# Moving sums of weights made in DRAM from the MLP into the attention, their copies issued by ScalarE, and two more direct pieces in the wide group

## The chip, the cores and the metric

The kernel runs on one NeuronCore of a Trainium2 chip. The core has five engines with an instruction stream each: TensorE (PE, matrix products into PSUM), VectorE (DVE), ScalarE (ACT), GpSimd (POOL) and SyncE (SP). An engine works through its own stream in the order in which it was written, and waits where an instruction needs something that another engine or a transfer has not finished. Sixteen DMA engines move data between DRAM and the on-chip memory SBUF, or from DRAM to DRAM; a transfer is issued by an instruction in the stream of SP, ScalarE or GpSimd. The metric is the time of one execution on the device in microseconds (us), as the median of several runs.

## The reference

One layer of an encoder on 256 tokens plus 16 meta tokens (272 rows, width 2048), all in float32:

```
h    = concat(meta_tokens, x)                                  # 272 x 2048
proj = rmsnorm(h) @ w_in                                       # 8 heads of neighbourhood attention + latent q, kv, rope key
out_a = neighbourhood_attention(q, k, v, bias)                 # 8 heads of 128
out_b = mla_attention(rmsnorm(cq) @ w_q_up, rmsnorm(ckv) @ w_kv_up, rope key)   # 8 heads
h    = h + concat(rmsnorm(out_a), rmsnorm(out_b)) @ w_out
y    = rmsnorm(h)
g    = conv3(y @ w_gate) + conv_b                              # depthwise over positions; 5632 columns
h    = h + (silu(g) * (y @ w_up)) @ w_down                     # 5632 -> 2048
return h[16:]                                                  # 256 x 2048
```

Every weight is read from DRAM once. The weights of `w_in`, `w_out`, `w_gate`, `w_up` and `w_down` are what streams through the chip.

## The kernel before, in words

**Products.** TensorE multiplies in a shortened float32 format (fp32r). So each weight piece is split by ScalarE into a rounded part (`whi`, L249, `split_hi`) and by VectorE into the rest (`wlo`, L253, `split_lo`), and an ordinary product is three matmuls: high by high, high by low, low by high (`mm3`, L712 to L714). In the up projection and in most of the direct down projection two instructions do the same work (`mm2`, L2035 and L2036).

**Pieces.** All weights form one list, `pieces`, in the order in which TensorE uses them. A piece is up to 128 x 1024 floats (512 KB). `load_weights` walks the list on SP's queue: it waits until one of a few raw buffers is free, and issues the load (L542). Then ScalarE splits, VectorE splits and frees the raw buffer, and TensorE uses the four high and four low buffers in turn. Pieces 0 to 15 belong to the compressed projections, then 16 pieces to each of four pairs of heads, then 32 to `w_out`, then the MLP. Piece 14 is the last but one of the first `w_in` columns, and piece 48 the first of the third pair of heads.

**Seven products for eight.** Parts of the MLP use a scheme of Strassen's kind: a 2 x 2 block product out of seven block products, where some factors are sums of weight quarters and some are sums of activation quarters. It is used for five groups of four column tiles of `w_up` (`QUADS`, 256 columns a product), for the first 1024 columns of `w_down` (the wide group, 512 columns a product, 22 row pairs of 21 matmuls each) and for the next 512 columns (the mid group, 256 columns a product). The remaining 512 columns of `w_down` are direct: four column tiles of six pieces each, 24 direct pieces, the last of each tile half as long.

The weight sums are mostly made by VectorE (`weight_sums`, L253 on `raw` and `halves`). For the wide group a part of them is made in DRAM: for each of the 22 row pairs `early` holds a DRAM buffer, one source to copy and one to add. The function `sums_in_dram` first copies the one source into the buffer, DRAM to DRAM (L542, on SP), then adds the other with an adding DMA issued by GpSimd (L781). Even pairs have 512 KB, odd ones 256 KB. When the wide group comes, these sums are loaded like weights (`early_sums`). `mlp_buffers` starts `sums_in_dram` when the MLP begins; a copy is issued each time round the loop and an addition two rounds behind it, and the loop then lets `EARLY_PACE`, 15 us of the plan's time, go by.

**Order of work.** The instruction streams are written by a planner inside the kernel (`Flow`). Each thread of work (a Python generator) asks for an engine and says how long it will hold it; the planner always takes the request that can start first, and so writes down one order for all engines. `yield "sp", 600` is such a request, `Event` and `Slots` are its waits. `dma_free` is the planner's idea of when the transfers are through. Only the order goes into the program. `fl.cur.t += x` moves the thread's planned time on, so its next request comes at least x ns later in the plan.

**Order of the MLP.** `work` lists the MLP's pieces: gate and up pieces with the five quads between them; then the mid group between the last gate and up pieces; then `TAIL`, a string of `m` (a row pair of the mid group) and `d` (a direct piece); then the wide group's units with direct pieces spread between them; and last, `BEHIND` direct pieces after the wide group. While the last ones run, `scheme_out` puts the wide group's seven results together on ScalarE, VectorE and GpSimd and writes them out.

Of the kernel before, what the change touches and what calls it, by code (L numbers as in the profile page):

```python
# [12 lines left out]
ALU = mybir.AluOpType  # L13
AX = mybir.AxisListType

P = 128
# [45 lines left out]
GATE_PRIO = 2  # L62
LENT = 14
MID_SUMS = 0
EARLY_PACE = 15000.0
LANDING, SAVING = 2600.0, 2500.0
BEHIND = 4
MID_LEAD, TAIL = 4, "mmdmmddddmmdddd"
LAST = FC // 2 - 1


# [145 lines left out]
def encoder_block(ctx: ExitStack, tc: tile.TileContext, io):  # L217
    nc = tc.nc
    ctx.enter_context(tc.manual_schedule())
    fl = Flow()  # L220
# [8 lines left out]
    def tiles(pool, n, shape, name, dt=F32):  # L229
        return [pool.tile(shape, dt, tag=f"{name}{i}", name=f"{name}{i}") for i in range(n)]  # L230


    def size(ap):
        n = 1
        for s in ap.shape[1:]:
            n *= s
        return n
# [194 lines left out]
    pieces = []  # L432
# [79 lines left out]
    def spread(a, b):  # L512
        out = []
        for i, u in enumerate(a):
            j, k = (t * len(b) // len(a) for t in (i, i + 1))
            out += [u] + b[j:k]
        return out
# [11 lines left out]
    work += [(left if c == "m" else ahead).pop(0) for c in TAIL]  # L529
    n = len(others) - BEHIND  # L530
    work += spread(scheme, others[AHEAD:n])
# [3 lines left out]
    dma_free = [0.0]  # L535

    def load(out, src, ev, queue):

        nc_bytes = 4 * P * size(out)
        t = max(dma_free[0], fl.cur.t) + nc_bytes / 350.0  # L540
        dma_free[0] = t
        queue.dma_start(out, src)  # L542
        fl.set(ev, t + (2000.0 if fl.cur.t < 4e5 else LANDING) - fl.cur.t)
# [3 lines left out]
    def load_piece():  # L547
        p = pieces[n_loads[0]]
        n_loads[0] += 1
        if isinstance(p, Quarters):  # L550
            if p is p.pair.pieces[0]:
                yield from load_pair(p.pair)
            return
        p.raw = yield from one(raws)
        yield "sp", 600
        load(p.raw[:, : p.n], p.src, p.loaded, nc.sync)
# [90 lines left out]
    def load_weights():  # L647
        while n_loads[0] < len(pieces):
            yield from load_piece()
# [102 lines left out]
    early_sums, early_mid, early = [], [], []  # L752
    for g in range(0, FC // 2 if MID_SUMS else 0, MID_SUMS or 1):
        n = min(MID_SUMS, FC // 2 - g)
        t = dpool.tile([P, n, PW // 4], F32, name=f"early_m{g}")
        w = io["w_down_m"][g : g + n].rearrange("g p c -> p g c")
        q, ev = PW // 4, Event()
        early.append((t, w[:, :, :q], w[:, :, 2 * q : 3 * q], ev))
        early_mid += [(t[:, i], ev) for i in range(n)]
    for g in range(FC // 2):  # L760
        ev, q, w = Event(), PW // 2, io["w_down_s"][g]
        if g % THIRD:
            t = dpool.tile([P, q], F32, name=f"early{g}")
            early.append((t, w[:, q : 2 * q], w[:, 2 * q : 3 * q], ev))
        else:
            t = dpool.tile([P, PW], F32, name=f"early{g}")
            early.append((t, w[:, : 2 * q], w[:, q : 3 * q], ev))
        early_sums.append((t, ev))

    def sums_in_dram():  # L770
        copied = [Event() for _ in early]
        for i in range(len(early) + 2):
            if i < len(early):
                t, src, _, _ = early[i]
                yield "sp", 600
                load(t, src, copied[i], nc.sync)
            if i >= 2:
                t, _, src, done = early[i - 2]
                yield copied[i - 2]
                yield "pool", 1000  # L780
                nc.gpsimd.dma_start(t, src, accum_op=ALU.add)  # L781
                dma_free[0] = max(dma_free[0], fl.cur.t) + 8 * P * size(t) / 350.0
                fl.set(done, 8000.0)
            fl.cur.t += EARLY_PACE

    late = [hpool.tile([P, 2, L], F32R, tag=f"late{i}", name=f"late{i}") for i in range(8)]
# [11 lines left out]
    def first_loads():  # L798
        k, first = 0, pieces[0]
        for n, weights in ((1, 1), (1, 1), (2, 2), (3, 2), (2, 1), (2, 1), (4, 2)):  # L800
            t = x_tiles[k // 8][:, k % 8 : k % 8 + n]
            yield "sp", 450
            ev = Event()
            load(t, io["xT"][:, k : k + n, :], ev, nc.sync)
            for i in range(n):
                xt[k], x_gain[k], ev_x[k] = t[:, i, :L], t[:, i, L:], ev
                k += 1
                fl.set(ev_xt[k - 1])
            if k == 1:
                yield "sp", 450  # L810
                part = first.parts[1]
                load(first.raw[:, part], first.src[:, part], first.there[1], nc.sync)
                k = 2
            for _ in range(weights):
                yield from load_piece()
        yield "sp", 600
        load(vecs, io["vecs"], ev_vecs, nc.sync)
        fl.spawn(load_weights())
        yield pieces[9].loaded
        yield "sp", 600  # L820
        load(consts, io["consts"], Event(), nc.sync)
        yield "sp", 600
        load(ident, io["ident"], ev_consts, nc.sync)
        yield "sp", 600
        load(mb, io["meta_bias"], Event(), nc.sync)

    def load_residual():
        yield ev_ob[HEADS - 1]
        for i in range(8):
            t = hpool.tile([P, 2, NT], F32, tag=f"late{i}", name=f"res{i}")  # L830
            yield "sp", 600
            hT[2 * i], hT[2 * i + 1] = t[:, 0, :], t[:, 1, :]
            load(t, io["xT"][:, 2 * i : 2 * i + 2, :NT], ev_res[i], nc.sync)
# [286 lines left out]
    for h in range(HEADS):  # L1120
        t = apool.tile([P, 2, NT], F32R, name=f"ob{h}")
        ob.append((t[:, 0, :], t[:, 1, :]))
        t = apool.tile([P, 2, NT], F32R, name=f"oa{h}") if h < 6 else hl[KC - HEADS + h]
# [647 lines left out]
    def attention_weights():  # L1771
# [76 lines left out]
        for parts, evs, evac in ((ob, ev_ob, out_b), (oa, ev_oa, out_a)):  # L1848
            for g in range(8):
# [7 lines left out]
                for c in range(2):  # L1857
                    fl.spawn(evac(2 * g + c, pss[c]))
        fl.spawn(scale_h())
        fl.spawn(mlp_buffers())  # L1860
        yield from mlp_weights()

# [4 lines left out]
    act = mts = None  # L1867

    def mlp_buffers():

        nonlocal act, mts
        yield ev_s2t
        yield ev_resT
        actx.close()
        mpool = ctx.enter_context(tc.tile_pool(name="mpool", bufs=1))
        act = mpool.tile([P, FC, 2, SEQ], F32R, name="act")
        mts = Slots(tiles(mpool, 12, [P, NT], "mt"))
        for t in tiles(mpool, 2, [P, PW], "sin"):
            fl.put(s_parts, t)
        for t in tiles(mpool, 1, [P, PW], "more_raw"):  # L1880
            fl.put(raws, t)
        for b in banks[4:]:
            fl.put(acc, b)
        for i in range(KC // 2):
            f = FC - KC + 2 * i
            near[i] = act[:, f : f + 2].rearrange("p f i t -> p (f i t)").bitcast(F32)
        fl.set(ev_mlp)
        fl.spawn(sums_in_dram())
        for i, (dst, saved) in enumerate(saved_sums["up"][:EARLY]):
            yield saved  # L1890
            yield "sp", 600
            load(near[i], dst, ev_near[i], nc.sync)
# [335 lines left out]
    def scheme_out(sums7):  # L2228
# [34 lines left out]
        fl.spawn(done(1, 0))  # L2263

    fl.spawn(first_loads())
    fl.spawn(make_gains())

# [171 lines left out]
```

## Time and profile before

| What | Value |
|---|---|
| Time, median of 3 runs | 1115.56 us (1112.71 to 1118.1) |
| The profiled execution: its time, its span | 1116.94 us, 1114.8 us |
| TensorE, VectorE, ScalarE, GpSimd busy | 1102.8, 1015.9, 751.8, 142.8 us |
| Moved by DMA | 265.35 MB, mean 238 GB/s |
| Attention and output projection | up to about 392 us |
| MLP with the five quads | about 397 to 784 us |
| Mid group, with the last gate and up pieces | about 784 to 950 us |
| Wide group | about 960 to 1098 us |
| First and last DRAM copy issued | 400.3 and 768.1 us |
| First and last DRAM addition issued | 407.1 and 776.7 us |

The span runs from the first to the last instruction, and the time of an execution is a little longer. Busy means that an instruction of the engine was under way; matmuls overlap, so the mean duration of one is longer than the distance to the next. In the groups' rows, `out<-in` are the program's names, `x` the count, and after the bar stand the busy time and the mean duration in ns. `[1.74 <-DMA raw<-in_w_up_s]` behind an instruction is the time that its engine stood idle before it, and what ended that. In waits, `A <- B: 7.0, 6, 2.0` means that A waited for B 7.0 us in all, 6 times, 2.0 us at the longest. SPq, ACTq and POOLq are the engines' instruction streams where they issue transfers.

### The profile page before, as it was taken

What the parts mean: (1) busy time and instruction counts of PE and PEld (TensorE: products, weight loads), DVE (VectorE), ACT (ScalarE), POOL (GpSimd) and SP (SyncE); (2) the same over time, 40 slices, a digit from 0 to 9 for tenths busy, and PEclk for the clock granted to TensorE, in tenths of its full rate; (3) what the DMA queues carried; (4) which work ended last, traced back from release to release, by engine and by line L of the source; (5) the groups of instructions that cost most, each with busy time, mean ns of one, the idle gap of its engine ahead of it and who ended that gap; (6) DMA issues with size and microseconds to landing.
All of it is one profiled execution on the core that took longest, in us unless ns stands there. A gap on an engine that the chain in (4) does not pass through costs nothing.

```text
span 1114.8 us, 22339 instructions
## 1 busy us (share of the span) xinstructions
PE 1102.8 (99%) x8164; PEld 1049.1 (94%) x8164; DVE 1015.9 (91%) x1922; ACT 751.8 (67%) x1514; POOL 142.8 (13%) x217
## 2 busy tenths in 40 slices
PE   9999999999999999999999999999999999999998
PEld 9999999999999999999999999999999999887777
DVE  7979888888878989999999999999999989899997
ACT  8788989898647786556656556666665665676664
POOL 3211222121332300000000000000000000310011
PEclk9999999999999999999999999999999999999999
DMA  9653434444655689778868878889889879698891
GB/s 318 197 174 121 151 123 156 139 155 140 225 185 171 216 308 306 250 244 244 288 196 268 253 239 267 284 253 316 296 295 304 269 271 360 241 316 298 296 315 75
DMA packets 82470, 265.35 MB, mean 238 GB/s; under 512 B 9304, under 2 KB 13016, under 8 KB 82360
## 3 DMA queue, kind: packets, MB, share of 16 engines
q1 hardware_dynamic: 78600, 254.08, 66.9%
q0 software_dynamic: 3472, 9.57, 4.9%
q8 instruction: 64, 1.05, 0.4%
q14 instruction: 46, 0.38, 0.1%
q10 hardware_dynamic: 288, 0.27, 0.1%
HBM read 245.39 MB, written 35.13 MB: 252 GB/s over the span
## 4 chain that ended last, share of the span: by engine, by line
PE 62%; DVE 21%; DMA 7%; ACT 5%; issue 4%; POOL 0%; SPq 0%; DVEq 0%; ACTq 0%; POOLq 0%
PE bank L289 14%; DVE wlo L253 12%; PE bank L714 11%; PE bank L712 11%; PE bank L713 11%; PE bank L2035 8%; PE bank L2036 4%; DMA raw<-in_w_up_s 3%; ACT whi L249 3%; DVE raw L253 2%; PE bank L295 2%; DVE mt L253 2%; DMA halves<-early 1%; DVE halves L253 1%; DVE mt L261 1%
## 5 line engine op out<-in xcount | busy, mean ns | idle before, releaser
L249 ACT ACTIVATE whi<-raw 128x512 fp32r<-128x512 f32 (+2 forms) x512 | 381.5, 766 | 159.9 <-PE bank L713 48.1
L253 DVE TENSOR_TENSOR wlo<-raw,whi 128x512 fp32r<-128x512 f32 (+2 forms) x512 | 443.5, 885 | 33.1 <-ACT whi L249 31.7
L712 PE MATMUL bank<-hl,whi 128*128 128x258 f32 (+1 forms) x1208 | 348.5, 289 | 0.1
L714 PE MATMUL bank<-hl,wlo 128*128 128x258 f32 (+1 forms) x1208 | 345.1, 286 | 1.4 <-DVE wlo L253 1.3
L713 PE MATMUL bank<-hl,whi 128*128 128x258 f32 (+1 forms) x1208 | 344.3, 285 | 0.0
L714 PEld LDWEIGHTS bank<-hl,wlo 128*128 128x128 f32 x1208 | 230.4, 191 | 3.5 <-DVE wlo L253 2.9
L713 PEld LDWEIGHTS bank<-hl,whi 128*128 128x128 f32 x1208 | 230.1, 190 | 0.1
L712 PEld LDWEIGHTS bank<-hl,whi 128*128 128x128 f32 x1208 | 229.2, 190 | 0.8 <-ACT scr L249 0.3
L289 PE MATMUL bank<-whi,act 128*128 128x256 f32 (+1 forms) x600 | 153.2, 306 | 0.6 <-ACT whi L249 0.6
L2035 PE MATMUL bank<-hl,whi 128*128 128x512 f32 x384 | 136.5, 395 | 0.0
L289 PEld LDWEIGHTS bank<-whi,act 128*128 128x128 f32 x600 | 105.1, 189 | 7.0 <-ACT whi L249 0.8
L2036 PE MATMUL bank<-hl,wlo 128*128 128x256 f32 x384 | 107.6, 280 | 0.0
L289 PE MATMUL bank<-wlo,act 128*128 128x256 f32 (+1 forms) x300 | 92.3, 308 | 1.4 <-DVE wlo L253 1.4
L2035 PEld LDWEIGHTS bank<-hl,whi 128*128 128x128 f32 x384 | 72.2, 188 | 14.8
L249 ACT ACTIVATE whi<-halves 128x1024 fp32r<-128x1024 f32 (+1 forms) x68 | 63.7, 948 | 32.3 <-PE bank L289 17.5
L253 DVE TENSOR_TENSOR wlo<-halves,whi 128x1024 fp32r<-128x1024 f32 (+1 forms) x68 | 74.1, 1113 | 4.2 <-ACT whi L249 4.2
L289 PE MATMUL bank<-whi,sin 128*128 128x256 f32 (+1 forms) x264 | 76.6, 333 | 0.0
L2036 PEld LDWEIGHTS bank<-hl,wlo 128*128 128x128 f32 x384 | 72.4, 188 | 0.0
L781 POOL DMA_DIRECT2D early<-in_w_down_s x22 | 18.2, 826 | 374.0 <-DMA early<-in_w_down_s 359.4
L249 ACT ACTIVATE whi<-more_raw 128x1024 fp32r<-128x1024 f32 (+2 forms) x59 | 49.6, 856 | 23.2 <-PE bank L2035 7.5
L289 PEld LDWEIGHTS bank<-wlo,act 128*128 128x128 f32 x300 | 56.7, 189 | 5.3 <-DVE wlo L253 2.2
L253 DVE TENSOR_TENSOR wlo<-more_raw,whi 128x1024 fp32r<-128x1024 f32 (+2 forms) x59 | 57.0, 980 | 2.0 <-ACT whi L249 2.0
(309 smaller groups left out, 2151.2 us busy)
## 6 DMA issues: line engine op xcount, KB each, us to landing
raw<-in_w_gate SPq DMA_DIRECT2D x71, 512.0 KB, 5.6
raw<-in_w_in SPq DMA_DIRECT2D x52, 512.0 KB, 4.0
raw<-in_w_up SPq DMA_DIRECT2D x42, 512.0 KB, 5.0
raw<-in_w_up_s SPq DMA_DIRECT2D x33, 512.0 KB, 6.1
raw<-in_w_out SPq DMA_DIRECT2D x32, 512.0 KB, 3.9
sin<-s_down SPq DMA_DIRECT2D x30, 512.0 KB, 7.1
s_down<-sums SPq DMA_DIRECT2D x22, 512.0 KB, 6.9
raw<-in_w_down_m SPq DMA_DIRECT2D x18, 512.0 KB, 6.2
```

The lines of the kernel that those rows point to most:

```text
L249: nc.scalar.activation(out, in_, f, **kw)
L253: nc.vector.tensor_tensor(out, a, b, op)
L261: nc.vector.scalar_tensor_tensor(out, a, s, b, op0, op1)
L289: nc.tensor.matmul(o, l, r, start=start, stop=stop)
L295: nc.tensor.transpose(o, i, ident[:n, :n])
L712: nc.tensor.matmul(ps, whi, xhi, start=start, stop=False)
L713: nc.tensor.matmul(ps, whi, xlo, start=False, stop=False)
L714: nc.tensor.matmul(ps, wlo, xhi, start=False, stop=stop)
L781: nc.gpsimd.dma_start(t, src, accum_op=ALU.add)
L2035: nc.tensor.matmul(ps, whi, x, start=start, stop=False)
L2036: nc.tensor.matmul(ps[:, :n], wlo, x[:, 0, :], start=False, stop=stop)
```

## The change

Three things change.

1. `sums_in_dram` is split in two. `copies_in_dram` issues the 22 copies, now in ScalarE's stream, with `COPY_PACE` (6 us of the plan) between them; it starts when piece 14 has landed in the plan. `sums_in_dram` keeps the 22 additions on GpSimd, each waiting for its copy, with an `EARLY_PACE` of 9.5 us; it starts when piece 48 has landed. Both are started from `first_loads`, and `mlp_buffers` no longer starts them.
2. `BEHIND` goes from 4 to 3: one direct piece less after the wide group.
3. `TAIL` loses its last `d`: one direct piece less ahead of the wide group. So 13 instead of 11 direct pieces are spread between the wide group's units.

What is computed is the same, and the same number of copies, additions, loads and matmuls is issued.

```diff
-EARLY_PACE = 15000.0
+EARLY_PACE = 9500.0
+COPY_PACE, COPY_AT, SUMS_AT = 6000.0, 14, 48
 LANDING, SAVING = 2600.0, 2500.0
-BEHIND = 4
-MID_LEAD, TAIL = 4, "mmdmmddddmmdddd"
+BEHIND = 3
+MID_LEAD, TAIL = 4, "mmdmmddddmmddd"
...
+    copied = [Event() for _ in early]
+
+    def copies_in_dram():
+        for (t, src, _, _), ev in zip(early, copied):
+            yield "act", 350
+            load(t, src, ev, nc.scalar)
+            fl.cur.t += COPY_PACE
+
     def sums_in_dram():
-        copied = [Event() for _ in early]
-        for i in range(len(early) + 2):
-            if i < len(early):
-                t, src, _, _ = early[i]
-                yield "sp", 600
-                load(t, src, copied[i], nc.sync)
-            if i >= 2:
-                t, _, src, done = early[i - 2]
-                yield copied[i - 2]
-                yield "pool", 1000
-                nc.gpsimd.dma_start(t, src, accum_op=ALU.add)
-                dma_free[0] = max(dma_free[0], fl.cur.t) + 8 * P * size(t) / 350.0
-                fl.set(done, 8000.0)
+        for (t, _, src, done), ev in zip(early, copied):
+            yield ev
+            yield "pool", 1000
+            nc.gpsimd.dma_start(t, src, accum_op=ALU.add)
+            dma_free[0] = max(dma_free[0], fl.cur.t) + 8 * P * size(t) / 350.0
+            fl.set(done, 8000.0)
             fl.cur.t += EARLY_PACE
...
+        yield pieces[COPY_AT].loaded
+        fl.spawn(copies_in_dram())
+        yield pieces[SUMS_AT].loaded
+        fl.spawn(sums_in_dram())
...
-        fl.spawn(sums_in_dram())
```

## The prediction, made before the result was known

> **What bounds the kernel now.** I read the page's busy shares first, then the chain that ended last, then busy time by stage, and in the stages with losses the waits and the transfers.
>
> ```profile
> span 1114.8 us, 22339 instructions
> PE 1102.8 (99%) x8164; PEld 1049.1 (94%) x8164; DVE 1015.9 (91%) x1922; ACT 751.8 (67%) x1514; POOL 142.8 (13%) x217
> PE 62%; DVE 21%; DMA 7%; ACT 5%; issue 4%; POOL 0%; SPq 0%; DVEq 0%; ACTq 0%; POOLq 0%
> ```
>
> TensorE is busy 99% of the span, so no change can save much: what it can save is the time in which TensorE waits for weights, or crawls. The chain says that the waits are behind VectorE (21%) and transfers (7%). Busy time by stage (columns: length, then busy us and instructions of TensorE, its weight loads, VectorE, ScalarE, GpSimd; granted clock; DMA share; GB/s) shows where:
>
> ```profile
> 30.00:170.00 140.00, 139.23 (x1134) 136.64 (x1133) 121.39 (x323) 114.66 (x348) 28.25 (x57) 1.00 0.47 154
> 170.00:392.00 222.00, 221.93 (x1841) 220.63 (x1840) 192.94 (x435) 167.46 (x447) 61.73 (x85) 1.00 0.54 173
> 397.00:784.00 387.00, 383.84 (x2967) 371.59 (x2966) 367.49 (x681) 239.46 (x386) 18.18 (x22) 1.00 0.84 265
> 784.00:950.00 166.00, 166.00 (x1212) 157.69 (x1211) 154.02 (x267) 100.00 (x156) 0.00 (x0) 1.00 0.87 300
> ...
> 960.30:1097.80 137.50, 134.89 (x618) 108.40 (x617) 132.50 (x145) 92.52 (x105) 15.33 (x14) 1.00 0.82 281
> ```
>
> The first two rows are attention and output projection: DMA half idle, TensorE full, ScalarE at 82% (114.66 of 140) in the first. The third is the first half of the MLP, with five quads of `w_up` columns by seven products: TensorE loses 3.2 us outright, VectorE is at 95%, the DMA at 0.84. The fourth, the mid group, has a DMA share of 0.87 and loses nothing. The fifth is the wide group. All 22 DRAM copies and 22 DRAM additions lie in the third row. Four stretches between the transposes that end the quads hold the same 168 matmuls of the scheme each, so their lengths can be compared:
>
> ```profile
> 491.10:557.90 66.80, 66.64 (x529) 65.06 (x528) 64.71 (x119) 41.18 (x66) 2.46 (x3) 1.00 0.81 251
> 557.90:627.30 69.40, 68.42 (x530) 65.76 (x529) 65.91 (x121) 41.13 (x67) 3.28 (x4) 1.00 0.81 248
> 627.30:698.15 70.85, 69.07 (x529) 66.80 (x527) 65.59 (x119) 42.27 (x67) 3.26 (x4) 0.98 0.78 242
> 698.15:766.34 68.19, 68.13 (x537) 66.32 (x535) 66.53 (x125) 42.83 (x69) 3.28 (x4) 1.00 0.87 282
> ```
>
> Against the first (66.80) the others lose 2.6, 4.05 and 1.4; the last has 8 matmuls more (66.80/529 = 0.126 each, 1.0), so 0.4. Together 7.0 us. Is that the DRAM traffic? The waits and transfers of the same stage (us in total, times, longest; then the queue and issue rows, the last number being us to landing), and one case in full:
>
> ```profile
> ACT whi L249 <- DMA raw<-in_w_gate: 7.9, 5, 3.4
> DVE raw L253 <- DMA raw<-in_w_up_s: 7.0, 6, 2.0
> ```
>
> ```profile
> q0 software_dynamic: 3167, 8.65, 13.7%
> ...
> raw<-in_w_up_s SPq DMA_DIRECT2D x33, 512.0 KB, 6.1
> ...
> early<-in_w_down_s POOLq DMA_DIRECT2D x11, 512.0 KB, 9.2
> ```
>
> ```profile
> 617.04 0.82 POOL L781 DMA_DIRECT2D early<-in_w_down_s  x1 [17.95 <-DMA early<-in_w_down_s]
> 619.06 0.33 SPq L542 DMA_DIRECT2D raw<-in_w_up_s  x1
> 628.64 0.69 DVE L253 TENSOR_TENSOR raw<-raw 128x512 f32<-128x512 f32 x1 [1.74 <-DMA raw<-in_w_up_s]
> ```
>
> An addition goes out at 617.04; the `w_up_s` load issued at 619.06 lands only at 628.6, 9.2 us after its issue where 6.1 is usual, and VectorE stands 1.74 us. VectorE has 5% to spare here, so what it loses comes back as a TensorE wait later, in the third quad.
>
> **The change, part by part.** *Copies and additions leave the MLP.* Removed from 397 to 784: 22 copies on SP's queue (0.50 us of SP each, in front of weight loads), and 22 additions on GpSimd, which has nothing else there. The additions alone are 13.7% of the DMA engines' time in this stage; the copies carry as many bytes on the other queue. Ends of this term: −7.0 (every quad at the first's 66.80) and +1.5 (the order written by the planner comes out differently in a stage that has 5% of VectorE to spare, nearest row the 1.4 between quads 1 and 4). I take −5.5, near the first end, since waits for transfers of up to 3.4 and 2.0 us stand in this stage, and the fourth row of stages, without DRAM sums, loses nothing even at 0.87.
>
> Part of the third quad's loss is the clock:
>
> ```profile
> 660.00:666.00 6.00, 5.02 (x27) 4.83 (x28) 5.89 (x9) 3.30 (x6) 0.00 (x0) 0.72 0.64 218
> ...
> 661.36 0.39 PE L289 MATMUL bank<-wlo,act 128*128 128x256 f32 x1 [0.88 <-DVE wlo L253]
> ```
>
> A granted clock of 0.72 over 6 us is 1.7 us lost, right behind a wait of 0.88 for a split that came late; I count it to that wait, so it goes when the wait goes.
>
> *The copies go to ScalarE's queue, from the landing of piece 14 on, at least 6 us apart in the plan.*
>
> ```profile
> 25.54 0.36 SPq L542 DMA_DIRECT2D raw<-in_w_in  x1
> 136.37 0.33 SPq L542 DMA_DIRECT2D raw<-in_w_q_up  x1
> L542 SPq DMA_DIRECT2D early<-in_w_down_s x22: 496/501/1727, 400.3 to 768.1; - x22
> L781 POOL DMA_DIRECT2D early<-in_w_down_s x22: 805/812/1011, 407.1 to 776.7; - x22
> 1.17 0.46 ACTq L1096 DMA_DIRECT2D pt<-in_xT  x1
> ```
>
> Piece 14 is issued at 25.54 and lands about 30; 22 × (6.0 + 0.35) = 140 us, so copies run from 30 to 170. An issue costs ScalarE 0.46 (its only comparable one) to 0.50 (SP's median for this very copy): 22 × 0.50 = 11.0 us, in the stage where it has 25.3 us idle. The copy waits for nothing; behind it on ScalarE stand splits of weights (whi) and softmax work, whose readers are VectorE and then TensorE. The chain between 28 and 168 tells how much of a delay there counts:
>
> ```profile
> by line: PE bank L712 12.1%; PE bank L714 12.0%; PE bank L713 11.9%; PE bank L289 9.5%; ACT whi L249 7.4%; issue 6.3%; DVE scr L261 5.8%; ACT scr L249 5.1%; DVE wlo L253 3.6%; PE bank L295 2.9%; DVE cols L269 2.1%; ACT mqr L249 2.0%; ACT qr
> 112.00:140.00 28.00, 27.76 (x232) 27.33 (x231) 25.08 (x68) 26.02 (x86) 6.66 (x15) 1.00 0.49 154
> ```
>
> ScalarE's shown lines make 14.5%, with the ones cut off about 18%: 11.0 × 0.18 = +2.0. Ends: 0 (all in idle time) and +11.0 (all on the path).
>
> *The additions go to GpSimd from piece 48 on.* It is issued at 136.37; 22 × (9.5 + 1.0) = 231 us, so about 141 to 372, long after each copy has landed, so GpSimd does not stand waiting. They cost 22 × 0.81 = 17.8 us on an engine that is busy 61.7 of 222. TensorE's waits for GpSimd there are small:
>
> ```profile
> PEld bank L289 <- POOL sq8r L277: 1.0, 3, 0.4
> ```
>
> If they doubled: +1.0. I take +0.3, floor 0.
>
> *The transfers collide with attention's weights instead.* Loads and splits go in one order, so a load can be matched to its first reader:
>
> ```profile
> raw<-in_w_in SPq DMA_DIRECT2D x48, 512.0 KB, 3.9
> 37.10 0.33 SPq L542 DMA_DIRECT2D raw<-in_w_in  x1
> 42.62 0.61 ACT L249 ACTIVATE whi<-raw 128x512 fp32r<-128x512 f32 x1
> 106.89 0.33 SPq L542 DMA_DIRECT2D raw<-in_w_in  x1
> 123.97 0.62 ACT L249 ACTIVATE whi<-raw 128x512 fp32r<-128x512 f32 x1
> ```
>
> A load lands in 3.9 us beside no DRAM sums and in 6.1 beside them. The one of 106.89 is read 17.1 us later: 13 us of cover. Without that cover each late load would cost up to 2.2; the thinnest place is 37.10, read 5.5 us later, cover 1.6, so 0.6 us at most. I take 0.
>
> *One direct piece moves from TAIL and one from BEHIND into the wide group* (13 between its units instead of 11). Nothing is added or removed.
>
> ```profile
> 936.62:947.93 11.31, 11.31 (x67) 9.81 (x65) 10.22 (x19) 4.73 (x8) 0.00 (x0) 1.00 0.85 308
> 960.34:970.08 9.74, 9.74 (x44) 7.89 (x43) 8.54 (x8) 8.49 (x11) 5.66 (x6) 1.00 0.47 164
> L253 DVE TENSOR_TENSOR wlo<-halves,whi 128x1024 fp32r<-128x1024 f32 x25 | 30.1, 1217 | 0.0
> ```
>
> The first row is four direct pieces: 2.83 us of TensorE each, against 1.2 of VectorE for the split: 1.6 us in which VectorE catches up. The second is a block of two row pairs, 9.74. The wide stage of 137.5 holds eleven such blocks (107.1) and nine and a half direct pieces (26.9): 134.0, so 3.5 us are lost. Two pieces more could return 2 × 1.6 = 3.2. But the one from TAIL gave the same slack just ahead, and is missed there: net of one, −1.5. Ends −3.2 and +1.6. At the end, `scheme_out` has 2.8 us less of direct work to hide behind:
>
> ```profile
> 1105.42 2.20 DVE L261 SCALAR_TENSOR_TENSOR raw<-raw,s,resT 128x256 f32<-128x256 f32 x4
> 1111.70 0.33 SPq L2024 DMA_DIRECT2D outT<-mt  x1
> ```
>
> VectorE is done with it at 1107.6, 4.1 us before the last output is issued; with 2.8 less it is still done first, so 0. If that cover went, about 1 us.
>
> **Sum.** −5.5 + 2.0 + 0.3 + 0 − 1.5 = −4.7. The profiled execution took 1116.94 (span 1114.8 and 2.1 around it), which would become 1112.2; it stands 1.4 above the median of the runs, 1115.56, so I forecast 1110.9. About 0.5% (5.6 us) is what a measurement of this kernel can tell from no change: below 1110.0 is faster, above 1121.1 slower.
>
> **Rivals.** *All of it is hidden* : ScalarE takes the copies in its 25.3 us of idle time, the quads come to 66.80: with the wide group's −1.5 that is −8.5, 1107.1. For it: idle time is more than twice the issue time. Against: 26.02 of 28 busy from 112 to 140.
>
> *ScalarE becomes the bound of attention (the slower side).* Between 112 and 140 the copies need 28/6.35 × 0.50 = 2.2 us and 2.0 are idle. If each copy delays TensorE by its whole issue, 11.0, the change is lost and more: −7.0 + 11.0 = +4.0, 1119.6. It decides from 7.0/22 = 0.32 us per copy; from (5.6 + 7.0)/22 = 0.57 us it is slower by 0.5%. SP's slowest issue of such a copy was 1.73, so a mean of 0.6 is possible, and that is the time I give it: −7.0 + 13.2 = +6.2, 1121.8. Against: the chain puts ScalarE at a fifth.
>
> *The quads' losses are not the DRAM sums'.* VectorE at 95% and an order written by the planner would lose them anyway: quads −1.5, the rest as above, +0.8 − 1.5 = −0.7, 1114.9. For it: the first quad has the same sums and loses nothing. Against: VectorE's 7.0 us of waits for `w_up_s`.
>
> *The queue makes no difference to the transfer.* Weight loads beside DRAM sums land in 6.1 instead of 3.9 whichever engine issues; if two copies overlap it is 2.2 more, 8.3, and the load of 37.10, read 5.5 us later, stalls its reader by 2.8: 1113.7. The Trainium skill (DMA: Bandwidth & Descriptors, section "Issuing engines are not separate DMA queues") has the rule behind it: all issuers share the same 16 engines and interleave, and another issuer saves only sequencer time. The trace agrees as far as it goes, with SP's and GpSimd's sums both beside loads of 6.1.
>
> **How the numbers follow.** Forecast (relief for the most part, a few us for ScalarE) 0.42, with its own range 1108 to 1113; about half of it is beyond 1110.0. All hidden 0.20, faster. Quads unchanged 0.15, same. The shared transfers 0.03, same. ScalarE the bound 0.20, slower. So faster 0.40, same 0.40, slower 0.20. The range goes from the two lower ends, 1115.56 − 7.0 − 3.2 = 1105.4, to the slow rival, 1121.8.
>
> **What would show it.** Right: no DRAM sums between 397 and 784, DMA share there 0.84 less the additions' 0.14 and something for the copies, about 0.65, `w_up_s` landing under 5 us, the four stretches within 1 us of each other, no stretch under full clock. ScalarE between 30 and 170 longer busy in issues, TensorE's lost time there (0.8 us in that row) up by about 2. Wide stage: waits for wlo down although two pieces longer. Wrong: TensorE idle before whi in attention, issues on ScalarE above 0.6 us, quads of 69 to 71 us with the sums gone, or an end where the last output waits for `scheme_out`.

## The result, and the profile after

The changed kernel takes 1108.79 us (median of 7 runs, 1107.92 to 1110.94) where the kernel before takes 1115.74 beside it: the ratio is 0.9942, 95% interval 0.9926 to 0.9958, so 7 us or 0.58% less, just over the half per cent that the prediction set as the least to be told from no change. The profiled execution took 1108.17, with a span of 1106.4, 8.4 shorter than before.

From the page of the changed kernel, its span, busy shares and the chain that ended last:

```profile
span 1106.4 us, 22329 instructions
PE 1096.7 (99%) x8164; PEld 1046.6 (95%) x8164; DVE 1017.9 (92%) x1922; ACT 751.6 (68%) x1514; POOL 149.5 (14%) x217
PE 90%; DVE 5%; ACT 2%; DMA 1%; issue 1%; SPq 0%; POOL 0%; ACTq 0%; DVEq 0%
```

All engines have the same number of instructions to do. What has shrunk is the part of the chain behind VectorE (21% to 5%) and transfers (7% to 1%). Busy time by stage, then in four stretches between the transposes that end the quads (columns as in the prediction):

```profile
30.00:170.00 140.00, 138.35 (x1127) 135.59 (x1125) 120.66 (x320) 114.71 (x346) 30.58 (x60) 1.00 0.71 215
170.00:392.00 222.00, 221.23 (x1835) 219.84 (x1834) 193.60 (x436) 165.14 (x446) 75.64 (x104) 1.00 0.74 209
397.00:784.00 387.00, 387.00 (x3021) 376.65 (x3020) 373.97 (x694) 244.94 (x396) 0.00 (x0) 1.00 0.68 227
```

```profile
491.21:557.86 66.65, 66.65 (x530) 65.24 (x529) 65.48 (x121) 42.19 (x67) 0.00 (x0) 1.00 0.65 214
557.86:624.69 66.83, 66.83 (x531) 65.30 (x529) 65.75 (x122) 41.55 (x67) 0.00 (x0) 1.00 0.64 213
624.69:691.51 66.82, 66.82 (x530) 65.31 (x529) 65.75 (x122) 41.61 (x67) 0.00 (x0) 1.00 0.66 220
691.51:758.36 66.85, 66.85 (x530) 65.33 (x529) 65.61 (x122) 41.59 (x67) 0.00 (x0) 1.00 0.71 237
```

In the MLP's first half TensorE is now never idle, the clock is full throughout, and the four stretches are within 0.2 us of each other: 267.15 together where they were 275.24. GpSimd has nothing there, and the DMA share fell from 0.84 to 0.68. In the attention it rose from 0.47 and 0.54 to 0.71 and 0.74. Transfers of the MLP's stage from 397 to 776, then those of the attention from 30 to 392 (KB each, median us to landing):

```profile
raw<-in_w_up_s SPq DMA_DIRECT2D x34, 512.0 KB, 4.6
```

```profile
q0 software_dynamic: 3168, 8.65, 15.7%
q10 hardware_dynamic: 3168, 8.65, 8.1%
...
raw<-in_w_in SPq DMA_DIRECT2D x47, 512.0 KB, 4.7
raw<-in_w_out SPq DMA_DIRECT2D x32, 512.0 KB, 5.8
early<-in_w_down_s POOLq DMA_DIRECT2D x11, 512.0 KB, 8.3
early<-in_w_down_s ACTq DMA_DIRECT2D x10, 512.0 KB, 5.6
...
scr<-scr SPq DMA_DIRECT2D x16, 32.2 KB, 5.0
```

The `w_up_s` loads land in 4.6 instead of 6.1. Attention's weights land later than before, `w_in` in 4.7 instead of 3.9 and `w_out` in 5.8 instead of 3.9, and no wait of ScalarE or VectorE for them is among the changed kernel's waits. How the sums themselves are issued (durations of the issue in ns, min/median/max; first and last start):

```profile
L543 ACTq DMA_DIRECT2D early<-in_w_down_s x22: 497/498/593, 28.5 to 172.3; - x22
L783 POOL DMA_DIRECT2D early<-in_w_down_s x22: 605/816/1024, 141.2 to 373.4; - x22
```

One row of each trace splits the gain: the matmuls of `mm_up`, with the start of the first and the last. The first comes when the attention is through; from the first to the last lie nearly all gate and up pieces, the quads and most of the mid group. First the kernel before, then the changed one:

```profile
L2035 PE MATMUL bank<-hl,whi x384: 388/392/485, 390.7 to 928.4; 128*128 128x512 f32 x192
```

```profile
L2040 PE MATMUL bank<-hl,whi x384: 388/392/485, 391.8 to 921.2; 128*128 128x512 f32 x192
```

Up to the first: 390.7 to 391.8, +1.1. From first to last: 537.7 to 529.4, −8.3. From the last to the end of the span: 186.4 to 185.2, −1.2. Together −8.4. I call these three attention, up stretch and rest, and read every run below by them. Each comes from one profiled execution. The one of the kernel before took 1116.94, 1.4 above the median of its runs, so −8.4 is somewhat more than the 7 of the medians.

### The profile page after: what moved, and what is told of

Same layout as the page of the kernel before. It is cut to its first block, busy times and chain, and to the rows that moved or that the text cites. A ratio compares the mean times of both kernels' runs of the same rounds, so it can differ in the third digit from the quotient of the medians.

```text
span 1106.4 us, 22329 instructions
## 1 busy us (share of the span) xinstructions
PE 1096.7 (99%) x8164; PEld 1046.6 (95%) x8164; DVE 1017.9 (92%) x1922; ACT 751.6 (68%) x1514; POOL 149.5 (14%) x217
## 4 chain that ended last, share of the span: by engine, by line
PE 90%; DVE 5%; ACT 2%; DMA 1%; issue 1%; SPq 0%; POOL 0%; ACTq 0%; DVEq 0%
PE bank L290 26%; PE bank L713 15%; PE bank L714 15%; PE bank L715 15%; PE bank L2040 11%; PE bank L2041 5%; DVE wlo L254 2%; PE bank L296 2%; DMA raw<-early 1%; DVE scr L262 1%; ACT whi L250 1%; ACT scr L250 1%; DMA scr<-scr 0%; DVE cols L270 0%; PE bank L845 0%
## 5 line engine op out<-in xcount | busy, mean ns | idle before, releaser
L254 DVE TENSOR_TENSOR wlo<-raw,whi 128x512 fp32r<-128x512 f32 (+2 forms) x513 | 448.4, 892 | 27.6 <-ACT whi L250 26.0
L278 POOL TENSOR_TENSOR mt<-mt,mt 128x256 f32<-128x256 f32 x3 | 13.5, 4490 | 645.4 <-ACT mt L250 645.4
```

The costliest lines, as they stand in the source:

```text
L254: nc.vector.tensor_tensor(out, a, b, op)
L278: nc.gpsimd.tensor_tensor(out, a, b, op)
```

## The experiments

The theory on trial is R: transfers of the DRAM sums make weight loads late, and that costs the quads their 8 us. The rivals are O (the order that the planner wrote costs them), P (the moved direct pieces carry the gain) and, for the price paid in the attention, S (the issue on ScalarE) against T (the transfers there). Ratios are to the kernel before on the same chip.

**The sums taken away, the order kept.** In the kernel before, planned as ever, copies and additions are not issued, and the wide group loads one of the two sources in place of their sum:

```diff
-        queue.dma_start(out, src)
+        queue and queue.dma_start(out, src)
...
-        early_sums.append((t, ev))
+        early_sums.append((early[-1][1], ev))
...
-                load(t, src, copied[i], nc.sync)
+                load(t, src, copied[i], None)
...
-                nc.gpsimd.dma_start(t, src, accum_op=ALU.add)
+                pass
```

> The kernel before with its order of work kept, but the 22 copies and 22 additions are not issued (the wide group loads the unsummed sources, so the sums are left out of the result). If the DRAM traffic itself costs the quads (theory R): the four stretches of the quads all come near 66.5 us, the time is about 1107 to 1108, some 8 below before, and a little below the changed kernel, since nothing is paid in the attention. If the quads lose by the order that the planner wrote (theory O): the order is the same, so 1114 to 1116 and stretches of 69 to 71 stay.

1108.22 us, ratio 0.9953 (0.9942 to 0.9965).

```profile
L2035 PE MATMUL bank<-hl,whi x384: 388/392/485, 390.2 to 920.2; 128*128 128x512 f32 x192
```

The up stretch is 530.0 instead of 537.7, with every compute instruction in its old place. Attention (390.2) and rest (185.8) hardly move. So 7.7 of the 8.3 us are the DRAM sums being in flight, and O is out for all but some 0.6. Even that is no more than the scatter, since the versions below without sums in the MLP have up stretches of 529.0 to 530.0. In whole times the difference is smaller, 5.2 (median 1108.22 beside 1113.40). One stretch of this run matters further on, the last between the quads' transposes:

```profile
690.36:758.09 67.73, 67.73 (x536) 66.20 (x535) 66.80 (x125) 42.73 (x69) 0.00 (x0) 1.00 0.70 238
```

**The sums brought back, the order kept.** The converse, in the changed kernel: as much traffic once more through the MLP, into buffers that nobody reads.

```diff
+    def traffic_in_mlp():
+        seen = []
+        for i in range(len(early) + 2):
+            if i < len(early):
+                t, src, _, _ = early[i]
+                yield "sp", 1
+                seen.append(dpool.tile([P, size(t)], F32, name=f"seen{i}"))
+                nc.sync.dma_start(seen[i], src)
+            if i >= 2:
+                yield "pool", 1
+                nc.gpsimd.dma_start(seen[i - 2], early[i - 2][2], accum_op=ALU.add)
+            fl.cur.t += 15000.0
...
         fl.set(ev_mlp)
+        fl.spawn(traffic_in_mlp())
```

> The changed kernel with its order of work kept, and beside it 22 more copies by SyncE and 22 more additions by GpSimd, into buffers that nobody reads, through the MLP at 15 us as before the change. R: the quads' losses come back, about 7 to 8 us, 1116. O: the order is that of the changed kernel, so it stays at 1109 with stretches within 1 us of each other.

1118.24 us, ratio 1.0049 (1.0032 to 1.0065): slower than the kernel before.

```profile
L2054 PE MATMUL bank<-hl,whi x384: 388/392/485, 391.1 to 929.6; 128*128 128x512 f32 x192
```

The up stretch is 538.5, so 9.1 come back. The waits of its stage from 397 to 784, which the changed kernel had at 2.0 us and less, are back as well:

```profile
ACT whi L250 <- DMA raw<-in_w_gate: 7.4, 7, 2.8
ACT whi L250 <- DMA raw<-in_w_up: 5.8, 6, 2.8
DVE raw L254 <- DMA raw<-in_w_up_s: 4.9, 5, 2.0
```

R holds in both directions. (The added traffic is a little denser than that of the kernel before: its copies lie from 400.6 to 735.1.)

**Copies alone in the MLP.** The same as the last one without its additions:

```diff
-                nc.gpsimd.dma_start(seen[i - 2], early[i - 2][2], accum_op=ALU.add)
+                pass
```

> The changed kernel with its order kept and 22 more copies by SyncE in the MLP, into buffers that nobody reads, at 15 us as before the change, but no additions there. Copies and additions together cost 9 us. If the additions carry it (13.7% of the DMA time and on a queue of their own): 1111, 2 to 3 us above the changed kernel. If the copies carry it (each stands on the queue of the weight loads, ahead of them): 1116.

1110.17 us, ratio 0.9964 (0.9951 to 0.9977).

```profile
L2054 PE MATMUL bank<-hl,whi x384: 388/392/485, 391.3 to 921.8; 128*128 128x512 f32 x192
```

An up stretch of 530.5: the copies cost 1.1, so 8.0 of the 9.1 come with the additions. The 1.1 is little more than the scatter (529.0 to 530.0 without sums in the MLP). That the additions weigh more fits the queue rows above: in the attention, for the same 8.65 MB, the additions hold the DMA engines 15.7% of the stage, the copies 8.1%.

**Additions alone in the MLP.** The copies stay in the attention, the additions go back.

```diff
-EARLY_PACE = 9500.0
+EARLY_PACE = 15000.0
...
-        yield pieces[SUMS_AT].loaded
-        fl.spawn(sums_in_dram())
...
         fl.set(ev_mlp)
+        fl.spawn(sums_in_dram())
```

> The changed kernel with the copies by ScalarE in the attention, but the additions in the MLP, 15 us apart as before the change. If it is the additions that make the weight loads late (13.7% of the DMA time, and the case shown had one in front of it): 5 to 6 of the 8 us come back, 1114. If it is the copies, which stand on SyncE's own queue ahead of the loads: 1110.

1144.23 us, ratio 1.0265 (1.0247 to 1.0283). I expected 1114. The issue row and GpSimd's timeline tell what happened:

```profile
L783 POOL DMA_DIRECT2D early<-in_w_down_s x22: 807/819/1428, 387.6 to 456.2; - x22
```

```profile
387.61 2.69 POOL L783 DMA_DIRECT2D early<-in_w_down_s  x3
396.48 0.83 POOL L783 DMA_DIRECT2D early<-in_w_down_s  x1 [6.18 <-issue]
399.65 0.81 POOL L783 DMA_DIRECT2D early<-in_w_down_s  x1 [2.34 <-issue]
403.41 0.81 POOL L783 DMA_DIRECT2D early<-in_w_down_s  x1 [2.94 <-issue]
```

The 15 us were never kept. A pace in the plan only sets the order; on the chip GpSimd goes through its stream as fast as it can, and here nothing stands between the additions, and their copies have long landed. All 22 went out within 69 us, some 3.3 apart. In the kernel before, each addition waited for a copy that was written between weight loads on SP, and that kept the pace; in the changed kernel the attention's work on GpSimd keeps it. The burst costs the stage from 400.78 to 526.19 dearly, with TensorE idle for 20 of 125 us and the clock down to 0.89:

```profile
400.78:526.19 125.41, 105.55 (x704) 97.82 (x705) 87.78 (x161) 61.35 (x100) 13.94 (x17) 0.89 0.86 252
```

So the run doesn't size the additions at the old pace (the two before it do that), but shows what they do when nothing spaces them.

**The sums without the pieces, the pieces without the sums.**

```diff
-BEHIND = 3
-MID_LEAD, TAIL = 4, "mmdmmddddmmddd"
+BEHIND = 4
+MID_LEAD, TAIL = 4, "mmdmmddddmmdddd"
```

> The changed kernel with TAIL and BEHIND as before: the sums moved, the direct pieces not. If the sums carry the gain: 1109 to 1111, the quads as in the changed kernel and the wide group 1 to 2 us longer. If the pieces carry it: 1115.

1108.89 us, ratio 0.9965 (0.9953 to 0.9977). And the kernel before with the new `BEHIND` and `TAIL`:

> The kernel before with the new TAIL and BEHIND: the direct pieces moved, the sums not. If the sums carry the gain: 1114 to 1115, the quads as before. If the pieces carry it: 1109 to 1110.

1114.63 us, ratio 1.0007 (0.9996 to 1.0017): no difference. P is out as the source of the gain. What the pieces are worth on top of the moved sums stays open within some 2 us: 0.9965 stands beside 0.9942 and, in a second measurement, 0.9950 with both, on other chips and with overlapping intervals. The wide stage itself, from its first to its last matmul with `sin`, in the changed kernel, in a second run of it, and in the run with the pieces alone:

```profile
950.24:1092.25 142.01, 139.80 (x658) 113.89 (x657) 136.98 (x150) 94.33 (x108) 24.86 (x15) 1.00 0.80 278
```

```profile
949.59:1092.92 143.33, 139.80 (x658) 113.94 (x657) 136.99 (x150) 94.29 (x108) 24.85 (x15) 1.00 0.80 275
```

```profile
956.44:1100.36 143.92, 139.84 (x658) 113.90 (x657) 137.02 (x150) 94.28 (x108) 24.84 (x15) 1.00 0.78 274
```

The same 658 matmuls take 142.0 to 143.9. TensorE stands idle in 2.2, 3.5 and 4.1 of that; before, in the row that the prediction shows, it stood 2.6 (137.50 less 134.89). So no gain from the pieces is to be seen in the wide stage. The rest is 186.4 before, 187.1 with the pieces alone, 185.2 and 186.5 in two runs of the changed kernel, which tells nothing apart either.

**What the attention pays: the changed kernel again, without sums, with copies by SP, with copies twice.** The changed kernel once more:

> The changed kernel itself, beside the others of this chip: 0.994 of before.

1109.78 us, ratio 0.9950 (0.9935 to 0.9965). In the second, copies and additions are not issued, by the same edits as in the first experiment:

> The changed kernel with its order of work kept, no copy and no addition issued (the sums are left out of the result). What is left to gain by hiding the sums better in the attention: by the prediction's terms 2.3 us, 1106.5 where the changed kernel takes 1109; if the attention hides them for nothing, no difference.

1108.34 us, ratio 0.9937 (0.9923 to 0.9951). In the third SP issues the copies:

```diff
-            yield "act", 350
-            load(t, src, ev, nc.scalar)
+            yield "sp", 600
+            load(t, src, ev, nc.sync)
```

> The changed kernel with the 22 copies issued by SyncE at the same places of the plan, and the order planned anew for that. If the issue on ScalarE costs what the prediction says, 2 us come back in the attention: some 1107 where the changed kernel takes 1109. If the cost there is that of the transfers, or none, the two are equal within 1 us.

1107.71 us, ratio 0.9934 (0.9920 to 0.9949). In the fourth ScalarE issues each copy a second time, into a buffer of its own:

```diff
+    again_s = []
...
             load(t, src, ev, nc.scalar)
+            again = dpool.tile([P, size(t)], F32, name=f"again{len(again_s)}")
+            again_s.append(again)
+            nc.scalar.dma_start(again, src)
```

> The changed kernel with each copy issued twice by ScalarE, the second into a buffer that nobody reads: 22 more issues of 0.5 us on ScalarE and 8.65 MB more, order kept. If ScalarE pays about 0.08 us of TensorE's time for each issue, as the difference to SyncE says: 2 us more than the changed kernel, 1111, lost in the attention. If the difference to SyncE was one of the order: no more than 0.5 us.

1114.60 us, ratio 1.0000 (0.9987 to 1.0013). The rows that tell the attention apart, of the changed kernel again, without sums, by SP, and twice:

```profile
L2040 PE MATMUL bank<-hl,whi x384: 388/392/485, 391.5 to 920.5; 128*128 128x512 f32 x192
```

```profile
L2040 PE MATMUL bank<-hl,whi x384: 388/392/485, 389.7 to 918.8; 128*128 128x512 f32 x192
```

```profile
L2040 PE MATMUL bank<-hl,whi x384: 388/392/485, 390.5 to 919.6; 128*128 128x512 f32 x192
```

```profile
L2045 PE MATMUL bank<-hl,whi x384: 388/392/485, 397.2 to 926.4; 128*128 128x512 f32 x192
```

The up stretch is 529.0 to 529.2 in all four. The attention ends at 391.5 to 391.8 with the sums and at 389.7 without: they cost it some 2 us, and with SP issuing 0.8. But that last difference is not firm: a version below with the very same attention, copies by SP, ends it at 391.3. And the run with the moved sums alone, whose attention is that of the changed kernel, ends it later than both:

```profile
L2040 PE MATMUL bank<-hl,whi x384: 388/392/485, 393.3 to 923.3; 128*128 128x512 f32 x192
```

In whole times the intervals of the changed kernel, of the one without sums and of the one with copies by SP overlap, so that only the traces could tell them apart, and for ScalarE against SP one trace of each does not. Doubling the copies costs 5.7 more in the attention (397.2 against 391.5), not 2. By itself that does not settle S against T: twice the copies are twice the issues and twice the traffic (the DMA share from 30 to 170 is 0.87).

What the waits name in the attention is not ScalarE's weight splits but `scr<-scr`. These are small transfers, 32 KB, on SP's queue. Their landing and the wait for them before, then the wait in the changed kernel, and the waits with copies twice:

```profile
scr<-scr SPq DMA_DIRECT2D x16, 32.2 KB, 2.4
DVE scr L253 <- DMA scr<-scr: 1.5, 1, 1.5
```

```profile
DVE scr L254 <- DMA scr<-scr: 3.5, 3, 1.5
```

```profile
POOL sum_b L278 <- DMA raw<-in_w_out: 8.7, 1, 8.7
DVE scr L254 <- DMA scr<-scr: 4.9, 3, 3.0
ACT scr L250 <- DMA raw<-in_w_in: 1.4, 1, 1.4
ACT scr L250 <- DMA early<-in_w_down_s: 1.0, 1, 1.0
```

They landed in 2.4 before and in 5.0 in the changed kernel. One place can be followed to TensorE, first in the changed kernel, then in the run with the sums alone (its TensorE row, and the 10 us around it):

```profile
73.69 0.43 DVE L254 TENSOR_TENSOR scr<-scr,consts 128x258 f32<-128x258 f32 x1 [1.09 <-DMA scr<-scr]
75.76 0.17 PE L290 MATMUL bank<-ones_r,sq8r 128*4 128x2 f32 x1 [0.79 <-DVE sq8r L266]
```

```profile
76.47 0.17 PE L290 MATMUL bank<-ones_r,sq8r 128*4 128x2 f32 x1 [1.24 <-DVE sq8r L266]
74.00:84.00 10.00, 8.46 (x58) 8.16 (x57) 9.42 (x24) 7.72 (x22) 2.10 (x4) 0.83 0.55 190
```

VectorE stands 1.09 us for the transfer, so `sq8r`, which it makes next for TensorE, comes late, and TensorE stands 0.79 us. Without the sums, the order being the same, neither wait is there. So T is shown for this place and some 0.8 of the 2 us. In the run with the sums alone the wait is 1.24 and TensorE's clock drops behind it: 0.83 over 10 us is 1.7 us lost, about what its attention ends later. With copies twice the wait is 1.46 and the clock 0.83 over the same 10 us, so 1.7 of the 5.7 are the clock's.

For S there is no such row. TensorE's own waits for ScalarE in the attention (1.0 us for `p` and 0.7 for `qraw` ahead of its weight loads) are as long without the sums as with them. With SP issuing, the `scr` transfers land no sooner (6.0, a wait of 3.3). What makes up the rest of the 2 us stays open: ScalarE's issues, GpSimd's, and other late transfers are not told apart.

**Two tries for a faster one, both with copies by SP.** All row pairs with two sums from DRAM:

```diff
-THIRD = 2
+THIRD = 1
```

> A try at a faster one: copies by SyncE, and all 22 row pairs with two sums made in DRAM instead of half of them, which takes eleven additions of 512 columns (0.6 us each, 6.6 us) from VectorE in the wide group and moves 2.9 MB more there. If VectorE bounds the wide group: its loss of 5 us goes to 2 to 3, 1105. If the loads do: it gets longer, 1108 to 1110.

1108.18 us, ratio 0.9943 (0.9930 to 0.9956). Its rest is the shortest of all, 183.5, but its attention ends at 392.9. Copies and additions are now all 512 KB, which may be why; in this one execution the attention takes back what the rest gains. And `TAIL` and `BEHIND` as before:

> Copies by SyncE with TAIL and BEHIND as before the change. If the two direct pieces are worth the 1.5 us of the prediction: 1109, 1.5 above the version with copies by SyncE. If they are worth nothing, as the kernel before with the pieces alone says: no difference.

1108.07 us, ratio 0.9942 (0.9929 to 0.9954), beside 0.9934 with the new ones: within the intervals. The version with copies by SP is the lowest of all, 1107.71, but not clear of the changed kernel (1109.78 beside it).

## Why the prediction was right, and where it was off

The time lay in the range and the direction was the forecast's; forecast were 4.7 us less, measured 7.0, and 8.4 in the profiled executions; the second measurement of the changed kernel gave 5.4 (1109.78 beside 1115.19). That the sum came so near is in part luck: the quads gave some 2.8 more than their term and the pieces' 1.5 never showed.

*The quads* were put at −5.5 with an end of −7.0, and measured −8.3. The mechanism stands, in both directions: the order held still and the traffic taken out, 7.7 go; the traffic put in, 9.1 come. The end of the term was right: the four stretches come to 267.15, which is four times the first quad's 66.80. Before they took 8.1 more; 1.0 of that was rightly taken off for eight more matmuls: with the old order and no sums the last stretch still has 536 of them and 67.73 us, and in the changed kernel the way from the last transposes to the end of the up stretch is 0.8 longer. The mis-sized steps are two. The 1.5 kept back for a loss by the planner's order ("nearest row the 1.4") was not needed: O is 0.6 at most. And the part ahead of the four stretches, which the sum left out, had its share too: before, 100.4 from the first `mm_up` (390.7) to the first transposes (491.1), after, 99.4 (391.8 to 491.2). The clock, counted to the late split, came back with it: 1.00 in every stretch.

*The rival that the losses were not the DRAM sums'* rested on the first quad, which has them and loses nothing. The runs without sums and with them again refute it. The argument that decided, VectorE waiting for a `w_up_s` load behind an addition, was the right row, and it even named the culprit: additions 8.0, copies 1.1.

*ScalarE* was put at +2.0 and GpSimd at +0.3; the attention got 1.1 longer (391.8 against 390.7), 0.8 in the second run, and against its own order without sums 2.1. The issue price of 0.50 was exact (median 498 ns, longest 593), ScalarE's busy time from 30 to 170, which does not count issues, stayed (114.66 to 114.71), and the rival with ScalarE as the bound, which needed 0.57 of TensorE's time for each copy, is far off. But the path was another, so that the size is luck. Late whi splits are not what TensorE waits for. The loss that can be followed comes by the small `scr` transfers, that is, by the collision of transfers, which was put at 0. That part looked at the weights' cover only, and there it was right: no wait for `w_in` or `w_out` on ScalarE or VectorE is among the changed kernel's waits. Its 3.9 against 6.1 for a load beside sums compared two stages. Within one stage it is 4.6 against 6.1 for `w_up_s`, and 3.9 against 4.7 for `w_in`.

*When the sums run* came out as worked out from pieces 14 and 48: copies 28.5 to 172.3 (said 30 to 170), additions 141.2 to 373.4 (said 141 to 372).

*The pieces* were put at −1.5. With the pieces alone the kernel is not faster (1.0007), and TensorE's idle time in the wide stage is 2.2 to 4.1 where it was 2.6. So the term is nearer 0. Its price was off as well: the 40 matmuls that the wide stage has more, two and a half pieces of 16, add 4.9 us to TensorE's busy time (134.89 to 139.80), 2.0 a piece and not 2.83, so there is less for VectorE to catch up in. The end did hold: the last output is issued after `scheme_out` is through, as said.

## What to carry to other kernels

A busy DMA need not cost anything: the mid group lost nothing at a share of 0.87, the quads lost 8 us at 0.84, where loads were late. Compare equal stretches of work with each other, and the loss has a number. When background transfers are moved, look at the cover of every transfer there: in the attention the weights had it (13 us for the load that the prediction followed), the small `scr` transfers had not. Whether cover or a less busy DMA made the attention the better place, no run separates. It is worth trying whether the traffic or the order is to blame by taking the one away and holding the other still. A pace given to a planner exists on the chip only if something in the same engine's stream, or a wait, enforces it.

## What the runs showed of the hardware that was not expected

An adding DMA from DRAM to DRAM takes about twice the time of the DMA engines that a copy of the same bytes takes here (15.7% against 8.1% of 362 us for 8.65 MB each), and 8.3 us to land where a copy of 512 KB takes 5.6. Spread through the MLP at one in some 16 us beside 22 copies, 22 of them cost 8.0 us of TensorE's time, and the copies alone 1.1. Written one after the other on an idle GpSimd they left it some 3.3 us apart, the fourth only after 6.2 us of standing for which the profile names no wait; that kernel was 29 us slower than the one before the change.

A short wait of TensorE can cost more than itself. In the attention a wait of 0.79 us left the granted clock full in the changed kernel; in the same program without the moved pieces the wait was 1.24 us, the clock fell to 0.83 over 10 us, and 1.7 us more were lost.
